# Clearing the result tiles of a block inversion on VectorE in place of GpSimd

## The chip, the cores and the metric

The kernel runs on one core of one Trainium2 chip. The metric is the device time of one execution in microseconds (us). The profile names the engines PE (TensorE), PEld (its weight loads), DVE (VectorE), ACT (ScalarE), POOL (GpSimd) and SP (SyncE, which here only issues DMAs); a q behind a name is the engine's sequencer, for example where it issues a DMA.

## What is computed

One layer of a hybrid encoder over 1024 tokens of width 1024: a windowed attention group and a bidirectional gated delta rule group read the same normalised input through one combined projection; their outputs are concatenated, projected and added; a feed-forward layer with squared ReLU follows.

```
xn   = rmsnorm(x);  proj = xn @ w_in                # q,k,v of attention; q,k,v,z,a,b of the delta rule
attn = windowed_gqa(q_a, k_a, v_a, bias, sink)      # 8 blocks of 128 queries, each sees 3 blocks of keys
gdn  = rmsnorm(rule(q,k,v,g,beta) + flip(rule(flip(...)))) * silu(z)
h    = x + concat(attn, gdn) @ w_out
out  = rmsnorm(h + relu(rmsnorm(h) @ w1)^2 @ w2)
# inside the rule, per chunk and head:
a_mat = strict_lower(beta * (k k^T) * decay)
t_mat = inverse(I + a_mat)                          # unit triangular
# t_mat multiplies the chunk's inputs; then a scan over the chunks carries a state
```

The inverses of these triangular matrices are what the changed line belongs to. There is one for every chunk, head and direction; the kernel works with 8 chunks of 128 tokens, 4 heads and 2 directions.

## The kernel before

All projections are products with the activations split in a high and a low part (`mm3`, lines L124 to L126: three matmuls for one product). The program is one list of phases. Inside a phase, `weave` interleaves two or more generators in the order in which the instructions are written down. That is not yet the order of execution: the program is built with `tile.TileContext(nc, schedule_with_timeline_sim=True)`, which lays out the queue of every engine by a simulated timeline and hands out tile buffers. On the chip each queue is then run strictly in its order, and an instruction that waits holds up all that stand behind it in its queue.

Tiles come from tagged pools with a fixed number of buffers. `pg` has 28 buffers of 128 x 1024 float32 and serves the activations, the bias tables and most of the inversion; `wh` and `wl` have three each, `pt` has 12 of half the size, and the PSUM tags `psA` and `psB` four banks each.

Two phases surround the change.

- The first weaves the rest of the input projection (`proj_conv` for v, `proj_z`, `proj_attn`) with the preparation of the delta rule: `prep` builds the matrices and stores them in DRAM (`atd`), `eliminate(0)` and `eliminate(1)` invert the 32 x 32 diagonal blocks of the forward and the backward direction on DVE (L675, L677), `diag_blocks` transposes the results (L686, L687: `ct` and `ctt`), and `invert(tt, (0, 1))` does the first two of four inversion steps.
- The second weaves `output()` (the attention, then the output projection) with `invert(tt, (2, 3))` and the two scans.

`proj_attn` begins with two casts that zero parts of the keys (L471). Each of its eight query products ends in `psA`; DVE moves it out (L494), ACT and GpSimd split it (L495, L496), and SP stores it to DRAM (`qad`, L500). `query` (L594) loads a block of queries back, by a DMA from GpSimd's queue. `bias_table` loads the attention's bias in 16 DMAs from SP's queue (L529). The scores of a block are the products of L544 and L545; DVE evicts them with the maximum (L546), ACT takes the exponentials (L558 and, for the sink, L555), and L559 is the next of DVE's small steps.

`invert` handles a pair of chunks in each step i, for both directions d (0 forward, 1 backward), in this order:

- per direction, load the matrices from `atd` (L707), take the result tile `tt[d][i]`, and clear it (L710). The result tile has the tag `pg`, except for the forward direction of i = 2 and 3, where it has `wh` and `wl`;
- ACT copies the inverted diagonal blocks into the cleared tile (L714, four copies for each direction);
- PE multiplies 32 x 32 blocks (L720), ACT moves the result (L723), PE multiplies again (L730, L734), and DVE writes the negated results into the tile (L739) and into `t64` (L746), for which ACT (L744) and GpSimd (L745) write the other parts;
- PE multiplies 64 x 64 blocks (L753), ACT moves the result (L755), PE multiplies again (L761), and DVE writes the last off-diagonal blocks (L764).

The scans read the finished tiles as the left operand of their products (L797). The clear is needed because the blocks above or below the diagonal are written by nobody else.

Of the kernel before, what the change touches and what calls it, by code (L numbers as in the profile page):

```python
# [77 lines left out]
class Block:  # L78
# [612 lines left out]
    def invert(self, tt, steps):  # L691


        nc = self.nc
        blk = lambda q: slice(32 * q, 32 * q + 32)
        ct, ctt = self.ct, self.ctt
        pairs = (((0, 1), (2, 3)), ((1, 0), (3, 2)))
        sub = ((0, 1), (3, 2))
        lo, hi = slice(0, 64), slice(64, 128)
        ends = ((lo, hi), (hi, lo))  # L700
        flat = lambda a: a.rearrange("p c h x -> p (c h) x")
        for i in steps:
            ns = slice(8 * i, 8 * i + 8)
            at = []
            for d in range(2):
                a = self.pg((P, 2, GH, P))
                nc.sync.dma_start(out=a, in_=self.atd[2 * i:2 * i + 2, :, d].rearrange("c p h x -> p c h x"))  # L707
                at.append(flat(a))
                tt[d][i] = self.pg((P, 2, GH, P)) if d or i < 2 else (self.wl if i % 2 else self.wh)((P, 2, GH, P), F32)
                nc.gpsimd.memset(tt[d][i].rearrange("p c h x -> p (c h x)"), 0.0)  # L710
            t = [flat(tt[d][i]) for d in range(2)]
            for d in range(2):
                for q in range(4):
                    nc.scalar.copy(out=t[d][blk(q), :, blk(q)], in_=ctt[d][blk(q), :, ns].rearrange("p x n -> p n x"))  # L714
            px = self.ps("psB", (P, 8, 32))
            for n in range(8):
                for j in range(2):
                    for d in range(2):
                        s, e = pairs[d][j]
                        nc.tensor.matmul(px[blk(e), n, :], at[d][blk(s), n, blk(e)], ct[d][blk(s), :, 8 * i + n],  # L720
                                         start=True, stop=True)
            x32 = self.pt((P, 8, 32))
            nc.scalar.copy(out=x32, in_=px)  # L723
            yield 1.4
            pyt, py = self.ps("psB", (P, 8, 32)), self.ps("psB", (P, 8, 32))
            for n in range(8):
                for j in range(2):
                    for d in range(2):
                        s, e = pairs[d][j]
                        nc.tensor.matmul(pyt[blk(s), n, :], x32[blk(e), n, :], ctt[d][blk(e), :, 8 * i + n],  # L730
                                         start=True, stop=True)
                for d in range(2):
                    e = sub[d][1]
                    nc.tensor.matmul(py[blk(e), n, :], ctt[d][blk(e), :, 8 * i + n], x32[blk(e), n, :],  # L734
                                     start=True, stop=True)
            t64 = self.pt((P, 8, 64))
            for d in range(2):
                for s, e in pairs[d]:
                    nc.vector.tensor_scalar(out=t[d][blk(s), :, blk(e)], in0=pyt[blk(s)], scalar1=-1.0, scalar2=None,  # L739
                                            op0=ALU.mult)  # L740
                a, b = sub[d]
                for q in (a, b):
                    c = slice(32 * (q % 2), 32 * (q % 2) + 32)
                    nc.scalar.copy(out=t64[blk(q), :, c], in_=ct[d][blk(q), :, ns].rearrange("p x n -> p n x"))  # L744
                nc.gpsimd.memset(t64[blk(a), :, 32 * (b % 2):32 * (b % 2) + 32], 0.0)  # L745
                nc.vector.tensor_scalar(out=t64[blk(b), :, 32 * (a % 2):32 * (a % 2) + 32], in0=py[blk(b)], scalar1=-1.0,  # L746
                                        scalar2=None, op0=ALU.mult)
            yield 2.4
            px = self.ps("psB", (P, 8, 64))
            for n in range(8):  # L750
                for d in range(2):
                    s, e = ends[d]
                    nc.tensor.matmul(px[e, n, :], at[d][s, n, e], t64[s, n, :], start=True, stop=True)  # L753
            xs = self.pt((P, 8, 64))
            nc.scalar.copy(out=xs, in_=px)  # L755
            yield 1.8
            py = self.ps("psB", (P, 8, 64))
            for n in range(8):
                for d in range(2):
                    s, e = ends[d]  # L760
                    nc.tensor.matmul(py[s, n, :], xs[e, n, :], t[d][e, n, e], start=True, stop=True)  # L761
            for d in range(2):
                s, e = ends[d]
                nc.vector.tensor_scalar(out=t[d][s, :, e], in0=py[s], scalar1=-1.0, scalar2=None, op0=ALU.mult)  # L764
            yield 1.8
# [612 lines left out]
```

## Time and profile before

| what | value |
|---|---|
| median of 3 runs | 1256.17 us (1255.85 to 1258.47) |
| the profiled execution | 1255.02 us |
| its span in the trace | 1253.3 us |
| mean granted TensorE clock | 0.983 |
| PE busy | 1191.6 us (95%) |
| DVE busy | 854.9 us (68%) |
| ACT busy | 621.4 us (50%) |
| POOL busy | 580.3 us (46%) |

The span runs from the first to the last instruction of the trace; the time of the execution is 1.7 us longer. Shares are averages over phases with different limits, so they do not say which engine is waited for in a given stretch. A wait in the trace is put down to the instruction that released it last. That instruction may itself have been held up by its queue, so a wait is followed back from engine to engine.

### The profile page before, as it was taken

To read this page: it belongs to the slowest core of one execution; us is meant where nothing else is said; L and a number is where in the kernel's file an instruction comes from. 1 tells how busy PE (TensorE), PEld (TensorE's weight loads), DVE (VectorE), ACT (ScalarE), POOL (GpSimd) and SP (SyncE) were. 2 spreads that over 40 slices of the span, in tenths; PEclk is the share of its full clock that TensorE was granted. 3 is DMA by queue.
4 is the path that set the end of the run, shared out by engine and by line. 5 is a ranking of instruction groups with operands and counts; after the bars stand their busy time and mean duration, and the time that the engine had idled before them with its cause. 6 is when DMAs were issued, how large, how long until landed. Compare 5 with 4: busy or idle time off the path is not lost.

```text
span 1253.3 us, 18527 instructions
## 1 busy us (share of the span) xinstructions
PE 1191.6 (95%) x6482; PEld 967.2 (77%) x6482; DVE 854.9 (68%) x1528; ACT 621.4 (50%) x1347; POOL 580.3 (46%) x488
## 2 busy tenths in 40 slices
PE   7999999899789989998999999999999999999997
PEld 5778777677568868877788888888777888888885
DVE  5667667982389986676655454544668797886976
ACT  6455688335485752125464554545545434444343
POOL 5354211362432433144573534535445665655595
PEclk9999999899889999998999999999999999999999
DMA  7134344441956678122234344443678624434323
GB/s 239 52 121 133 101 171 140 139 126 40 223 168 158 190 216 296 60 84 85 84 131 159 132 151 143 154 159 134 223 280 280 223 85 167 151 121 148 95 90 135
DMA packets 121630, 187.62 MB, mean 150 GB/s; under 512 B 11043, under 2 KB 64416, under 8 KB 121537
## 3 DMA queue, kind: packets, MB, share of 16 engines
q1 hardware_dynamic: 96708, 152.58, 37.9%
q10 hardware_dynamic: 16381, 29.67, 6.3%
q0 software_dynamic: 8448, 4.20, 1.9%
q8 instruction: 51, 0.84, 0.3%
q14 instruction: 42, 0.34, 0.1%
HBM read 122.39 MB, written 63.49 MB: 148 GB/s over the span
## 4 chain that ended last, share of the span: by engine, by line
PE 49%; DVE 6%; DMA 3%; issue 2%; POOL 1%; ACT 1%; ACTq 0%; POOLq 0%; DVEq 0%; SPq 0%
PE psA L124 8%; PE psA L125 8%; PE psA L126 8%; PE psB L126 7%; PE psB L125 7%; PE psB L124 7%; DMA pg<-sd 3%; PE psB L797 2%; DVE pg L1154 1%; DVE pt L1163 1%; DVE wr L1166 1%; PE psB L209 1%; DVE pg L1199 1%; DMA sd<-pt 0%; DVE wr L1161 0%
## 5 line engine op out<-in xcount | busy, mean ns | idle before, releaser
L124 PE MATMUL psA<-pg,wh 128*128 128x512 f32 x416 | 167.6, 404 | 2.1 <-ACT pt L458 2.1
L126 PE MATMUL psA<-pg,wl 128*128 128x512 f32 x416 | 166.9, 401 | 0.0
L125 PE MATMUL psA<-pg,wh 128*128 128x512 f32 x416 | 166.5, 400 | 0.0
L120 POOL TENSOR_TENSOR wl<-wr,wh 128x512 fp32r<-128x512 f32 x44 | 70.2, 1618 | 154.0 <-ACT wh L119 153.9
L1154 DVE TENSOR_TENSOR pg<-pg 128x512 fp32r<-128x512 f32 x112 | 122.7, 1127 | 18.8 <-ACT pg L1153 18.6
L120 POOL TENSOR_TENSOR wh<-wr,wh 128x512 fp32r<-128x512 f32 x32 | 47.9, 1518 | 131.5 <-ACT wh L119 131.5
L1071 ACT ACTIVATE pt<-pt 128x512 f32<-128x512 f32 x64 | 40.4, 632 | 122.7 <-DVE pt L1061 122.7
L125 PE MATMUL psA<-pg,pg 128*128 128x512 f32 x256 | 99.7, 391 | 0.5 <-POOL pg L120 0.5
L124 PE MATMUL psA<-pg,pg 128*128 128x512 f32 x256 | 99.0, 391 | 1.0 <-DVE pg L1199 1.0
L126 PE MATMUL psA<-pg,pg 128*128 128x512 f32 x256 | 99.7, 389 | 0.0
L120 POOL TENSOR_TENSOR pg<-wr,pg 128x512 fp32r<-128x512 f32 x48 | 73.4, 1560 | 51.0 <-ACT pg L119 51.0
L124 PEld LDWEIGHTS psA<-pg,wh 128*128 128x128 f32 x416 | 79.2, 190 | 21.3 <-ACT pt L458 2.4
L125 PEld LDWEIGHTS psA<-pg,wh 128*128 128x128 f32 x416 | 79.3, 191 | 19.7 <-issue 0.9
L126 PEld LDWEIGHTS psA<-pg,wl 128*128 128x128 f32 x416 | 79.1, 190 | 18.6
L1153 ACT CAST pg<-pg 128x512 fp32r<-128x512 f32 x112 | 67.2, 620 | 41.3 <-DMA pg<-sd 31.0
L126 PE MATMUL psB<-pg,pg 128*128 128x512 f32 x192 | 75.0, 390 | 1.3 <-DVE pg L1154 1.3
L125 PE MATMUL psB<-pg,pg 128*128 128x512 f32 x192 | 75.0, 391 | 0.8 <-POOL pg L120 0.7
L124 PE MATMUL psB<-pg,pg 128*128 128x512 f32 x192 | 74.7, 390 | 0.4 <-ACT pg L1153 0.4
L119 ACT CAST wh<-wr 128x512 fp32r<-128x512 f32 x76 | 43.6, 623 | 45.5 <-PE psA L125 24.8
L1061 DVE TENSOR_TENSOR pt<-psB,pt 128x512 f32<-128x512 f32 x39 | 26.9, 689 | 55.1 <-PE psB L126 30.1
L1061 DVE TENSOR_TENSOR pt<-psA,pt 128x512 f32<-128x512 f32 x39 | 26.8, 689 | 55.0 <-PE psA L126 39.5
L124 PEld LDWEIGHTS psA<-pg,pg 128*128 128x128 f32 x256 | 48.0, 188 | 12.6 <-DVE pg L1199 2.3
(385 smaller groups left out, 3307.7 us busy)
## 6 DMA issues: line engine op xcount, KB each, us to landing
sd<-pt ACTq DMA_DIRECT2D x112, 256.0 KB, 2.2
pg<-sd SPq DMA_DIRECT2D x112, 256.0 KB, 2.9
wr<-in_w_ffn_in SPq DMA_DIRECT2D x32, 512.0 KB, 3.8
wr<-in_w_in SPq DMA_DIRECT2D x22, 512.0 KB, 4.8
pg<-in_x SPq DMA_DIRECT2D x16, 512.0 KB, 5.4
wr<-in_w_ffn_out SPq DMA_DIRECT2D x16, 512.0 KB, 4.8
sc<-kvd SPq DMA_DIRECT2D x14, 512.0 KB, 4.1
kvd<-pt SPq DMA_DIRECT2D x16, 256.0 KB, 2.8
```

Of the source, the lines that this page charges most:

```text
L119: nc.scalar.copy(out=h, in_=raw)
L120: (eng or nc.gpsimd).tensor_tensor(out=l, in0=raw, in1=h.bitcast(F32), op=ALU.subtract)
L124: nc.tensor.matmul(ps, wh, xh, start=first, stop=False, skip_group_check=onto)
L125: nc.tensor.matmul(ps, wh, xl, start=False, stop=False, skip_group_check=onto)
L126: nc.tensor.matmul(ps, wl, xh, start=False, stop=last, skip_group_check=onto)
L209: self.nc.tensor.transpose(ps[:, i * P:(i + 1) * P], row[:, k * P:(k + 1) * P], self.ident)
L797: nc.tensor.matmul(ps[:, h - g.start, :], left(h), right[:, h, :], start=True, stop=True)
L1061: self.nc.vector.tensor_tensor(out=out, in0=in0, in1=in1, op=ALU.add)
L1071: self.nc.scalar.activation(out=c, in_=c, func=AF.Relu)
L1153: nc.scalar.copy(out=s[:, 0], in_=raw)
L1154: v.tensor_tensor(out=s[:, 1], in0=raw, in1=s[:, 0].bitcast(F32), op=ALU.subtract)
L1163: v.tensor_tensor(out=b["T2"], in0=b["B22"], in1=b["T1"], op=ALU.subtract)
```

## The change

The eight clears of L710 are issued on DVE (`nc.vector`) in place of GpSimd (`nc.gpsimd`). Tiles, sizes and everything else stay as they are.

```diff
--- before.py
+++ after.py
@@ -707,7 +707,7 @@
                 nc.sync.dma_start(out=a, in_=self.atd[2 * i:2 * i + 2, :, d].rearrange("c p h x -> p c h x"))
                 at.append(flat(a))
                 tt[d][i] = self.pg((P, 2, GH, P)) if d or i < 2 else (self.wl if i % 2 else self.wh)((P, 2, GH, P), F32)
-                nc.gpsimd.memset(tt[d][i].rearrange("p c h x -> p (c h x)"), 0.0)
+                nc.vector.memset(tt[d][i].rearrange("p c h x -> p (c h x)"), 0.0)
             t = [flat(tt[d][i]) for d in range(2)]
             for d in range(2):
                 for q in range(4):
```

## The prediction

> **What bounds the kernel now.** I read the page first, then the busy windows, then the waits of PE, and only then the line that the diff touches. From the page: the span, the engines' busy times and the chain that ended last.
>
> ```profile
> span 1253.3 us, 18527 instructions
> PE 1191.6 (95%) x6482; PEld 967.2 (77%) x6482; DVE 854.9 (68%) x1528; ACT 621.4 (50%) x1347; POOL 580.3 (46%) x488
> PE 49%; DVE 6%; DMA 3%; issue 2%; POOL 1%; ACT 1%; ACTq 0%; POOLq 0%; DVEq 0%; SPq 0%
> ```
>
> PE is busy for 1191.6 of 1253.3 us, so about 62 us of the span are PE waiting, and a change on other engines is worth what it takes from or adds to those 62 us. The next lines are the clears by their source line (buffer, count, shortest, median and longest in ns, first and last start in us, shape).
>
> ```profile
> L710 POOL MEMSET pg<- x6: 954/964/1088, 263.0 to 346.5; 128x1024 f32 x6
> L710 POOLq EVENT_SEMAPHORE  x1: 17/17/17, 295.5 to 295.5; - x1
> L710 POOL MEMSET wh<- x1: 957/957/957, 301.6 to 301.6; 128x1024 f32 x1
> L710 POOL MEMSET wl<- x1: 957/957/957, 302.5 to 302.5; 128x1024 f32 x1
> ```
>
> Eight clears of about 0.96 us, 7.7 us of GpSimd in all, and GpSimd is at 46%: its time is not what matters. What matters is who stands behind them. The waits of PE, asked for the stretch in which the inversion runs (total us, times, longest):
>
> ```profile
> PE psB L761 <- ACT pt L755: 4.9, 2, 4.4
> PE psB L753 <- DVE pt L746: 3.1, 3, 2.2
> PE psB L720 <- DMA pg<-atd: 3.1, 2, 2.1
> PE psB L720 <- DVE sc L687: 1.6, 1, 1.6
> ...
> PE psA L544 <- DMA pt<-qad: 0.8, 1, 0.8
> ```
>
> The longest, 4.4 us, names ACT, but ACT was only passing on a wait. The timelines of the four engines around it, in the order POOL, DVE, ACT, PE, SP (start, duration, engine, line, and in brackets the idle time before):
>
> ```profile
> 316.94 1.00 POOL L594 DMA_DIRECT2D pt<-qad  x1 [3.89 <-DMA pg<-biasd]
> 317.95 0.97 POOL L710 MEMSET pg<- 128x1024 f32 x1
> ```
>
> ```profile
> 312.06 0.87 DVE L746 TENSOR_SCALAR pt<-psB 32x256 f32<-32x256 f32 x2
> 318.95 0.88 DVE L739 TENSOR_SCALAR pg<-psB 32x256 f32<-32x256 f32 x2 [6.02 <-POOL pg L710]
> 319.86 2.49 DVE L494 TENSOR_SCALAR pt<-psA 128x512 f32<-128x512 f32 x4
> ```
>
> ```profile
> 318.95 2.51 ACT L714 COPY pg<-sc 32x256 f32<-32x256 f32 x4 [7.32 <-POOL pg L710]
> 321.48 0.59 ACT L755 COPY pt<-psB 128x512 f32<-128x512 f32 x1
> 322.09 2.18 ACT L495 CAST pt<-pt 128x512 fp32r<-128x512 f32 x4
> ```
>
> ```profile
> 322.12 1.68 PE L761 MATMUL psB<-pg,pt 64*64 64x64 f32 x32 [4.36 <-ACT pt L755]
> ```
>
> ```profile
> 311.65 2.73 SPq L500 DMA_DIRECT2D qad<-pt  x4
> 314.48 7.28 SPq L529 DMA_DIRECT2D pg<-biasd  x14
> 322.74 11.30 SPq L500 DMA_DIRECT2D qad<-pt  x16
> ```
>
> The reader is to see one chain. The clear of the backward tile of step i=1 stands on GpSimd behind the query load of L594, which waits 3.89 us for DMAs that have nothing to do with the inversion. Only after the clear, at 318.95, can ACT copy the diagonal blocks (L714, idle 7.32 us before) and DVE write its blocks (L739, idle 6.02 us), and behind these stand L755, for which PE waits, and four PSUM evictions (L494).
>
> **The change part by part.**
>
> *Off GpSimd.* 6 x 0.964 + 2 x 0.957 = 7.7 us. The DMA descriptors and subtractions behind them move up by at most 1 us each. Worth nothing by itself: no wait of PE in the rows above is on POOL.
>
> *On DVE.* The trace has no clear on DVE. Two rows bound it: 0.96 us, what GpSimd takes, and 1.19 us, half of the 2.38 us of two casts on DVE that write 1024 elements per partition (L471, below). I take 1.19, the nearer row because it is DVE's own; eight make 9.5 us. The Trainium skill, page "VectorE: DVE Perf Modes", section "Zero memsets can be issued as uint32 (trn2)", says that a memset takes one cycle per element whatever the type; with the 0.96 GHz of the page "Trainium Kernel Development and Optimization", section "NeuronCore Architecture", that would be an estimated 1.07 us, and 8.5 us for the eight. No run here has shown it yet.
>
> Where these 9.5 us fall is read from busy windows (PE, PEld, DVE, ACT, POOL busy, with counts, granted clock, DMA share, GB/s) and a few rows of DVE and POOL:
>
> ```profile
> 264.00:282.00 18.00, 16.52 (x74) 12.82 (x72) 17.65 (x27) 8.93 (x15) 9.18 (x9) 1.00 0.24 74
> 293.00:302.00 9.00, 9.00 (x71) 6.70 (x71) 0.36 (x1) 4.80 (x8) 5.13 (x5) 1.00 0.33 102
> 336.00:343.00 7.00, 3.00 (x74) 2.37 (x73) 4.00 (x11) 5.26 (x9) 6.41 (x9) 0.76 1.11 309
> 343.00:545.00 202.00, 187.89 (x1516) 156.55 (x1517) 165.79 (x518) 102.86 (x301) 66.73 (x58) 0.97 0.58 175
> ```
>
> ```profile
> 268.69 2.38 DVE L471 CAST pg<-zero 64x1024 fp32r<-64x1024 f32 x2
> ...
> 280.21 1.87 DVE L687 STREAM_TRANSPOSE sc<-sc 128x1024 f32<-128x1024 f32 x1
> ...
> 349.42 0.16 DVE L559 TENSOR_TENSOR nm<-nm,nm 128x4 f32<-128x4 f32 x1 [1.11 <-ACT nm L555]
> ```
>
> ```profile
> 264.95 0.96 POOL L710 MEMSET pg<- 128x1024 f32 x1 [1.00 <-DVE pt L675]
> ...
> 297.62 0.96 POOL L710 MEMSET pg<- 128x1024 f32 x1
> ```
>
> (a) *Two clears of step i=0* (the first and the second, at 263.0 and 264.95). DVE is busy for 17.65 of 18 us there with the elimination, whose last transpose (L687) ends at 280.21 + 1.87 = 282.08 and releases PE's first L720. Two clears ahead of it move it by up to 2 x 1.19 = 2.4 us; the bounds are 0 and +2.4. I take 0: PE has the projection products to run in the meantime, and the order of the queues is laid out anew with the clears in it (the trace already shows DVE running things out of the program's order, with the casts of L471 in the middle of the elimination). That cover is gone if PE's order stays as it is; then the wait of 1.6 us becomes 4.0.
>
> (b) *Three clears of i=1, 2 and 3, forward* (at 297.6, 301.6 and 302.5 on GpSimd). DVE is busy for 0.36 of 9 us at that place: 0. They can push L764 by a clear or so; its result is first read in the scan.
>
> (c) *The clear of i=1, backward.* DVE is free at 312.06 + 0.87 = 312.93. The clear also needs its buffer to be free; the trace shows no wait for that at 317.95, and the bias loads, which take buffers of the same tag and come later in the program, go out at 314.48. I take 314.5 as the latest likely time. Then the clear ends at 315.7, L714 at 315.7 + 2.51 = 318.2, L755 at 318.8, and L761 runs at about 318.85 in place of 322.12: 3.3 us. Bounds: 3.7 with the buffer at 312.9 (L755 must still wait for PE's products, which end at 322.12 - 4.36 = 317.76, and takes 0.59), 0 with the buffer at 317.9.
>
> (d) *What is late next.* After L761 come two projection products and then the score products and the L720 of step i=2, and these wait for DMAs: the `atd` loads (3.1 us of PE waiting) and the second query load (0.8). Both hang on SP's queue, and that queue is nearly full: the 14 bias loads end at 314.48 + 7.28 = 321.76, the 16 query stores start at 322.74. Earlier evictions let the stores start 0.98 us sooner, no more. At 0.68 us each (2.73 / 4, the first four) instead of 11.30 / 16 = 0.71 they save another 0.4 us; at the 0.52 of the bias loads (7.28 / 14) 3.0 more. So of 3.3 us gained at 322 between 1.0 and 3.3 are left at 342; I take 1.2, next to the stores' own rate. The rest reappears as a longer wait of L720 for `atd`: some 5 us in place of 3.1.
>
> (e) *The last two clears* (i=2 and 3, backward) (the last at 346.5) fall among the first attention blocks. One ahead of L746, which PE waits 2.2 us for, costs up to 1.2; but DVE idles 1.11 us just ahead of it, waiting for ACT's exponentials (L555). These start earlier, since the first score block comes up to 3.3 us sooner. Bounds +1.2 and -2.2; I take the hole as filled by the clear (+0.1) and half of the 2.2 us wait as gone (-1.1): -1.0.
>
> Sum: 0 + 0 - 1.2 - 1.0 = -2.2 us. The profiled execution took 1255.02 us (span 1253.3), so it would become 1252.8; the median of the runs shown, 1256.17, lies 1.15 above it, and I forecast on that: 1254.0. All of it is at the edge of what can be told from no change: 0.2% is 2.5 us.
>
> **The rivals.**
>
> *R1, the gain is kept whole.* If SP's order is laid out differently, so that stores and `atd` loads follow the earlier evictions, nothing is given back: -3.7 - 2.2 = -5.9, 1250.3. For it: the wait is real and it is a wait for a queue, not for data. Against it: SP's full queue from 314 to 334.
>
> *R2, nothing happens.* The buffer comes free only just before 317.9, or `atd` and the queries land no sooner (the DMA share is 1.11 in 336 to 343), so the whole 4.4 us turns into a DMA wait: 1256.2. Against it: the bias loads' buffers.
>
> *R3, the elimination pays.* (a) at its upper bound, DVE having no room: 1254.0 + 2.4 = 1256.4. For it: 17.65 of 18. Against it: other PE work at that place. The Trainium skill, page "Perfetto Trace Analysis", section "Optimizing Scalar/DVE Operations", says that where DVE is saturated, work may go from it to another engine, even GpSimd; by that rule this change goes the wrong way in that stretch, and the 17.65 us agree that DVE is saturated there.
>
> *R4, slower by a new order.* The program is laid out by a simulated timeline, so eight instructions that change engine can permute everything behind them. The place is the attention and scan stretch: PE idles 202.00 - 187.89 = 14.1 us there, mostly behind DVE, which is busy for 165.79. A third more idling (+4.7) outweighs -2.2 by 2.5 us and decides for slower; half more, +7.1, gives 1261.1. For it: chains of small DVE instructions with PE behind them. Against it: no row says which way a new order goes; it can also gain.
>
> **How the numbers follow.** My case 0.46 (its own range 1252.0 to 1255.5, about half of it beyond 0.2%), R1 0.16, R2 0.07, R3 0.06, R4 0.25. Faster by over 0.2%: 0.22 + 0.16 = 0.38. Within: 0.24 + 0.07 + 0.06 = 0.37. Slower: 0.25. The range runs from a little beyond R1 to R4: 1249.5 to 1261.0.
>
> **What would show it.** (c) is right if ACT's L714 of i=1 waits under 3 us for the clear and PE's wait for L755 falls from 4.4 to about 1 us. (d) is right if PE's wait for the `atd` loads grows. (a) is wrong if the wait for L687 grows from 1.6 towards 4. A clear on DVE that takes longer than 1.19 us would upset (a) and (e). The prediction fails if the order of PE's products between 260 and 545 is another one: then the rows above do not carry over.

## The result, and the profile after

| kernel | median | profiled execution | its span | mean granted clock |
|---|---|---|---|---|
| before | 1256.01 us (1254.44 to 1258.47, 4 runs) | 1255.02 us | 1253.3 us | 0.983 |
| after | 1262.96 us (1261.73 to 1264.01, 4 runs) | 1262.11 us | 1260.4 us | 0.981 |

The change makes the kernel slower: the ratio is 1.0054, with a 95% interval of 1.0037 to 1.0071, some 6.8 us. The page of after begins

```profile
span 1260.4 us, 18524 instructions
PE 1191.3 (95%) x6482; PEld 965.4 (77%) x6482; DVE 852.9 (68%) x1536; ACT 621.7 (49%) x1347; POOL 571.5 (45%) x480
```

PE is busy about as long as before (1191.3 against 1191.6 us), so in the sum the 7.1 us by which the span grew stand as PE waiting. The sum hides that some products took longer and others less; that comes below. DVE has eight instructions more, and yet its busy time did not grow. The six clears with the tag `pg`:

```profile
L710 DVE MEMSET pg<- x6: 912/912/912, 272.3 to 349.7; 128x1024 f32 x6
```

0.912 us each, shorter than on GpSimd (0.964). Now the waits of PE in the stretch where the inversion runs (260 to 420 us), which before held 4.9 us for L755 and 3.1 us for `atd`:

```profile
PE psB L720 <- DMA pg<-atd: 8.1, 2, 7.2
PE psA L585 <- ACT pt L575: 5.1, 2, 2.8
PE psA L544 <- ACT pt L575: 1.5, 1, 1.5
...
PE psB L761 <- ACT pt L755: 1.0, 2, 0.7
PE psB L753 <- DVE pt L746: 0.8, 1, 0.8
```

The wait at which the change was aimed went from 4.4 to 0.7 us, that for L746 from 2.2 to 0.8, and that for L687 is gone from the list. In their place stand a longer wait for `atd` and more waits for L575. Most of the waits for L575 hang on the last clear, that of i=3 backward. Before, GpSimd made it at 346.50; on DVE it stands among the rows of the attention and runs at 349.70. ACT's four copies into the tile (L714) wait for it, and the copies L575, for which PE waits, stand behind them in ACT's queue, which then has no gap up to the L575 of 359.86. ACT's timeline, of before and then of after:

```profile
349.30 2.54 ACT L714 COPY pg<-sc 32x256 f32<-32x256 f32 x4
```

```profile
350.65 2.61 ACT L714 COPY pg<-sc 32x256 f32<-32x256 f32 x4 [0.49 <-DVE pg L710]
353.29 0.58 ACT L575 COPY pt<-psA 128x512 f32<-128x512 f32 x1
```

From 341 to 380 PE waits 4.3 us for L575 in after, and not at all in before. (The other 2.3 us fall between 380 and 415 and are no matter of the clears: the kernel e4 below, with none moved, has 2.3 us there, too.) The timelines of DVE and PE around the clear of i=1 backward show what became of the wait that the change was aimed at:

```profile
311.88 0.91 DVE L710 MEMSET pg<- 128x1024 f32 x1 [0.28 <-issue]
```

```profile
317.50 1.15 PE L761 MATMUL psB<-pg,pt 64*64 64x64 f32 x32 [0.74 <-ACT pt L755]
...
338.56 0.28 PE L720 MATMUL psB<-pg,pg 32*32 32x32 f32 x2 [7.21 <-DMA pg<-atd]
```

The clear is done at 312.8 in place of 318.9, L761 starts 4.62 us earlier (322.12 before), and 20 us later L720 of step i=2 starts at 338.56 where it started at 339.60: only 1.04 us of it are left. The reason is SP's queue:

```profile
314.54 6.68 SPq L529 DMA_DIRECT2D pg<-biasd  x14
321.32 11.18 SPq L500 DMA_DIRECT2D qad<-pt  x16
332.54 1.06 SPq L529 DMA_DIRECT2D pg<-biasd  x2
333.70 0.89 SPq L707 DMA_DIRECT2D pg<-atd  x2
```

SP issues with hardly a pause: 14 bias loads, 16 query stores of 0.70 us each on average, two more bias loads, and only then the two loads for which L720 waits.

So much for the place of the change. The loss is 250 us further on. The waits of PE from 420 to 640 us, of before and then of after:

```profile
PE psA L910 <- DVE wr L907: 1.0, 2, 0.7
```

```profile
PE psA L910 <- DVE wr L907: 5.3, 3, 4.3
```

L910, the transposes of `out_gdn`, had not been touched. PE's timeline there, of before:

```profile
582.97 6.51 PE L209 MATMUL psB<-ident,pg 128*128 128x128 f32 x32 [3.59 <-DVE pg L205]
589.46 0.66 PE L910 MATMUL psA<-ident,wr 128*128 128x128 f32 x4
589.87 0.47 PE L124 MATMUL psA<-pg,pt 128*128 128x512 f32 x1
...
592.28 0.39 PE L125 MATMUL psA<-pg,pt 128*128 128x512 f32 x1
```

and of after:

```profile
583.59 6.25 PE L209 MATMUL psB<-ident,pg 128*128 128x128 f32 x32 [3.58 <-DVE pg L205]
594.14 1.11 PE L910 MATMUL psA<-ident,wr 128*128 128x128 f32 x4 [4.30 <-DVE wr L907]
594.91 0.78 PE L124 MATMUL psA<-pg,pt 128*128 128x512 f32 x1
...
599.21 0.39 PE L125 MATMUL psA<-pg,pt 128*128 128x512 f32 x1
```

At L209 after is 0.62 us late: over inversion, attention and scans together the change brought nothing and cost at most that in these two executions. At L910 it is 4.68 us late, and at the last row (592.28 and 599.21) 6.93. What came on top behind L910 is the clock: the ten products from that L124 to that L125 take 2.41 us before and 4.30 us after. The busy window from 592 to 596 (PE, PEld, DVE, ACT, POOL busy, granted clock, DMA share, GB/s), of before and of after, shows it:

```profile
592.00:596.00 4.00, 4.00 (x19) 3.21 (x19) 3.43 (x5) 1.24 (x2) 2.98 (x2) 1.00 0.55 152
```

```profile
592.00:596.00 4.00, 1.86 (x7) 1.67 (x8) 2.79 (x5) 0.77 (x2) 2.26 (x2) 0.53 0.01 2
```

Around and after the idle 4.30 us PE was granted 0.53 of its clock. The Trainium skill, page "TensorE: Matmul & The Clock Gate", section "Why this matters for your kernels", says that an idle gap of more than about 3 us drops PE back to half its clock; the 4.30 us and the 0.53 agree. Both kernels show the same once just ahead of this place: behind the wait of 3.59 us (3.58 in after) at L209 the granted clock was 0.50 from 583 to 587. So the loss is 4.06 us of lateness at L910 (4.68 less the 0.62 from L209), 0.36 in its own transposes (589.46 to 589.87 against 594.14 to 594.91), and 1.89 in the ten products: 6.31 us, of which the last two terms are slow clock, and nothing is made good afterwards.

Why L907 comes late is seen in the chain behind it. `out_gdn` of the last chunk takes the squares of four heads on ACT (L900), makes a factor of them in four small steps on DVE (L902 to L905), a power on GpSimd (L906), scales on DVE (L907), and PE transposes (L910). Beside it, the next phase's pass over the tokens already issues its large instructions (L966 and L214 on ACT, L215, L970 and L950 on DVE). The last square on ACT, and the first and the last small step on DVE, of before:

```profile
584.71 0.30 ACT L900 ACTIVATE scr<-pg 128x128 f32<-128x128 f32 x1
```

```profile
585.13 0.17 DVE L902 TENSOR_TENSOR sm<-sm,sq 128x4 f32<-128x4 f32 x1 [0.75 <-ACT scr L900]
...
586.38 0.15 DVE L905 TENSOR_TENSOR sm<-sm,sq 128x4 f32<-128x4 f32 x1
```

and of after:

```profile
586.45 0.69 ACT L966 ACTIVATE pg<-psB,cols 128x512 f32<-128x512 f32 x1 [0.15 <-PE psB L209]
587.03 0.30 ACT L900 ACTIVATE scr<-pg 128x128 f32<-128x128 f32 x1
```

```profile
587.65 0.15 DVE L902 TENSOR_TENSOR sm<-sm,sq 128x4 f32<-128x4 f32 x1
...
591.41 0.16 DVE L905 TENSOR_TENSOR sm<-sm,sq 128x4 f32<-128x4 f32 x1
```

The last square, which in before stands behind the first L966, stands behind the second one in after, and that waits for PE: 587.03 in place of 584.71. DVE's four small steps then stand between large ones of the token pass and take from 587.65 to 591.41, 3.76 us in place of 1.25. Nothing there is slower by itself: the queues of ACT and DVE were laid out in another order. Before had next to no room for it. Its L907,

```profile
588.73 0.68 DVE L907 TENSOR_TENSOR wr<-pg,sm 128x512 f32<-128x512 f32 x1
```

ended at 589.41, 0.05 us ahead of L910.

### The profile page after: what moved, and what is told of

Same layout as the page of the kernel before. It is cut to its first block, busy times and chain, and to the rows that moved or that the text cites. A ratio compares the mean times of both kernels' runs of the same rounds, so it can differ in the third digit from the quotient of the medians.

```text
span 1260.4 us, 18524 instructions
## 1 busy us (share of the span) xinstructions
PE 1191.3 (95%) x6482; PEld 965.4 (77%) x6482; DVE 852.9 (68%) x1536; ACT 621.7 (49%) x1347; POOL 571.5 (45%) x480
## 4 chain that ended last, share of the span: by engine, by line
PE 49%; DVE 6%; issue 3%; DMA 2%; POOL 2%; ACT 1%; POOLq 0%; ACTq 0%; DVEq 0%
PE psA L124 9%; PE psA L125 9%; PE psA L126 9%; PE psB L125 7%; PE psB L124 7%; PE psB L126 7%; PE psB L797 2%; POOL pg L120 1%; DMA pg<-sd 1%; DVE pt L1163 1%; DVE pg L1199 1%; DVE wr L1166 1%; DMA sc<-in_w_ffn_out 1%; DVE pg L215 0%; DVE pg L1154 0%
## 5 line engine op out<-in xcount | busy, mean ns | idle before, releaser
L124 PE MATMUL psA<-pg,wh 128*128 128x512 f32 x416 | 167.2, 403 | 2.2 <-ACT pt L458 2.2
L125 PE MATMUL psA<-pg,wh 128*128 128x512 f32 x416 | 166.0, 399 | 0.0
L125 PE MATMUL psA<-pg,pg 128*128 128x512 f32 x256 | 99.8, 391 | 1.7 <-POOL pg L120 1.7
L124 PE MATMUL psA<-pg,pg 128*128 128x512 f32 x256 | 99.0, 391 | 1.5 <-DVE pg L1199 0.9
L124 PEld LDWEIGHTS psA<-pg,wh 128*128 128x128 f32 x416 | 79.0, 190 | 21.2 <-ACT pt L458 2.4
L125 PEld LDWEIGHTS psA<-pg,wh 128*128 128x128 f32 x416 | 78.9, 190 | 19.5 <-issue 0.9
L125 PE MATMUL psB<-pg,pg 128*128 128x512 f32 x192 | 75.2, 391 | 0.8 <-POOL pg L120 0.7
L124 PE MATMUL psB<-pg,pg 128*128 128x512 f32 x192 | 74.7, 390 | 0.2 <-ACT pg L1153 0.2
L124 PEld LDWEIGHTS psA<-pg,pg 128*128 128x128 f32 x256 | 48.0, 188 | 13.1 <-DVE pg L1199 2.2
```

What stands on the lines that cost most here:

```text
L124: nc.tensor.matmul(ps, wh, xh, start=first, stop=False, skip_group_check=onto)
L125: nc.tensor.matmul(ps, wh, xl, start=False, stop=False, skip_group_check=onto)
```

## The experiments

The theory T1: the loss is the new order of `out_gdn`'s last chunk, which the simulated timeline lays out when times shift anywhere ahead of it; the clears on DVE cost nothing. The rival T2: the clears cost it themselves, by DVE's time. Ratios are to before as it was timed beside them, each with its 95% interval. Its median there was 1258.37 us for e1 to e4, 1258.03 for e5 to e8 and 1257.61 for e9 to e12, against 1256.01 in the table above, so it is the ratios, and not the medians, that can be compared over these groups.

**e1, one clear on DVE, that of i=1 backward.**

```diff
-                nc.gpsimd.memset(tt[d][i]...
+                (nc.vector if (i,d)==(1,1) else nc.gpsimd).memset(tt[d][i]...
```

> Kernel before, with one of the eight clears, that of i=1 backward, on DVE; PE and ACT issue in the order of before. T1 (the loss is the new order of the last chunk's out_gdn chain alone): PE's wait at L761 falls from 4.4 us to under 1, PE ends the projection some 5 us earlier, L720 then waits 5 to 7 us for atd behind SP's full queue, PE L910 has no wait at 590, and the time is that of before, 1256, at most 1 us under it. Rival, the local gain is kept: 1252. T2 (a clear on DVE costs its own 0.9 us of DVE's time): 1257.

Measured 1255.34 us, ratio 0.9984 (0.9971 to 0.9998). PE's waits from 260 to 420:

```profile
PE psB L720 <- DMA pg<-atd: 7.5, 2, 6.4
PE psB L761 <- ACT pt L755: 2.4, 3, 1.1
```

The wait at L761 is 1.1 us at most, that for `atd` grew to 6.4, and about 2 us are kept (0.16%), a little more than T1 said. This part of the change, alone, is a small gain.

**e2, one clear on DVE, that of i=3 backward** (the same edit with `(3,1)`).

> Kernel before, with the clear of i=3 backward alone on DVE. The order at the end of the inversion then comes out as after the whole change. T1: PE L910 waits about 4 us for DVE L907 near 590 us, and the time is about 6 us over before, 1262. T2 (a clear on DVE costs its own time on DVE): at most 0.9 us over before, 1257, with no wait at L910.

Measured 1267.14 us, ratio 1.0079 (1.0059 to 1.0100). PE's timeline:

```profile
587.39 2.82 PE L209 MATMUL psB<-ident,pg 128*128 128x128 f32 x12 [3.58 <-DVE pg L205]
...
597.95 1.12 PE L910 MATMUL psA<-ident,wr 128*128 128x128 f32 x4 [4.29 <-DVE wr L907]
```

The same wait of 4.3 us for L907, from a single clear that runs 240 us ahead of it. T2 would allow 0.9 us. L910 starts 10.56 us after that L209 row; in before it was 6.49, so 4.07 us are lost between the two, as in after. The whole, some 10 us, is more than the 6 that T1 gave. The traces show where the rest lies: at that L209 row e2 is already 4.42 us late (587.39 against 582.97). L720 of i=2, ahead of the moved clear, is 1.13 late (340.73 against 339.60), and the remaining 3.3 are lost behind it. A part of them is the clear's own. It runs on DVE at 354.14, and ACT's copies behind it start 5.8 us later than the 349.30 of before:

```profile
355.08 2.61 ACT L714 COPY pg<-sc 32x256 f32<-32x256 f32 x4 [0.40 <-DVE pg L710]
```

From 341 to 380 PE then waits 2.0 us for L575, in before not at all. So T1 is too strong where it says that the clears cost nothing: this one costs PE time at its own place as well, through what waits for it and not through DVE's 0.9 us.

**e3, after with one more ordering.** The first L966 of the token pass is put behind the last square of `out_gdn` on ACT; the clears stay on DVE.

```diff
-            nc.scalar.activation(out=scr, in_=o[:, h, :], func=AF.Square, accum_out=so[:, h:h + 1])
+            self.square = nc.scalar.activation(out=scr, in_=o[:, h, :], func=AF.Square, accum_out=so[:, h:h + 1]).ins
...
-            nc.scalar.activation(out=b12, in_=ps, func=AF.Copy, scale=self.w_ffn[:, k:k + 1])
+            first = nc.scalar.activation(out=b12, in_=ps, func=AF.Copy, scale=self.w_ffn[:, k:k + 1]).ins
+            k or self.tc.add_manual_dep(first, self.square.name, ...)
```

> Kernel after, all eight clears on DVE, with one more ordering: the first L966 of the token pass is put behind the last square (L900) of out_gdn on ACT. T1: the 4.3 us wait of PE L910 is gone or under 1 us, and the time is within 1 us of before, 1255 to 1257. T2 (the clears on DVE cost the loss themselves): stays at 1262 to 1263.

Measured 1257.87 us, ratio 0.9998 (0.9985 to 1.0011): the loss is gone. PE's timeline:

```profile
589.48 0.60 PE L910 MATMUL psA<-ident,wr 128*128 128x128 f32 x4
```

L910 starts with no wait, though all eight clears are on DVE. T2 falls as the cause of the loss. The order is not that of before, where the first L966 stands ahead of the last square; it is another good one.

**e4, before with the same ordering**, the control.

> Kernel before with the same ordering of L966 behind L900, the clears on GpSimd: the control of the run above. T1: its order there is as good as before, so 1255 to 1257. If the ordering by itself gained some 6 us (1250), the run of after with it would say nothing on T1.

Measured 1258.18 us, ratio 0.9998 (0.9984 to 1.0012). The ordering by itself is worth nothing where the order was good already; in e3 it was worth the 0.54%.

**e9, the order without any moved clear.** The clears are on GpSimd as before, and every second query store is issued by ACT's queue (`(nc.sync, nc.scalar)[g].dma_start` in L500), which shifts the simulated times too. Its partner e8 has the same stores and the ordering of e4.

> Kernel of e4 (clears on GpSimd) with every second query store on ACT's queue: control of e7. T1: PE's wait at L761 for the clear on GpSimd stays at 4 us or becomes shorter only if the query loads ahead of the clear on GpSimd's queue, which wait for these stores, come earlier; the time is 0 to 2 us under e4's 1258.2.

> Kernel of e8 without the ordering of L966 behind L900: every clear on GpSimd as before, every second query store on ACT's queue. The planner then puts the last two squares of out_gdn's last chunk behind ACT's L966, as in after, though no clear is moved. T1 (the order alone costs): PE L910 waits about 4 us near 590, and the time is 5 to 7 us over e8's 1258.5, about 1264. T2 (the clears on DVE are needed for the loss): as e8, 1258 to 1259.

Measured e8 1258.53 us, 1.0008 (0.9995 to 1.0020), and e9 1262.61 us, 1.0037 (1.0023 to 1.0052). PE's timeline of e9:

```profile
595.09 0.98 PE L910 MATMUL psA<-ident,wr 128*128 128x128 f32 x4 [4.27 <-DVE wr L907]
```

The wait for L907 is there again, with GpSimd clearing all eight tiles. It costs 0.29% against e8 by the ratios, 3.7 us (the two were timed in different groups), less than the 5 to 7 us expected. So the clears on DVE are neither needed for the loss (e9) nor enough for it (e1, e3).

**e10, four clears on DVE**, those of i=0 and 1 in both directions (the condition `i<2`; the word "forward" in its name is wrong), with no ordering by hand.

> Kernel before with four of the eight clears on DVE, those of i=0 and 1, and nothing ordered by hand; the end of the inversion keeps the order of before. T1: no wait of PE L910, and the time is that of before or 1 to 2 us under it, as in e1: 1255 to 1257. T2 (each clear on DVE costs 0.9 us): 3 to 4 us over before, about 1261.

Measured 1255.49 us, ratio 0.9978 (0.9966 to 0.9989). PE's timeline:

```profile
589.90 0.66 PE L910 MATMUL psA<-ident,wr 128*128 128x128 f32 x4
```

No wait at L910, and a gain of 0.22%, 2.8 us, a little more than T1 gave, where T2 gave a loss of 3 to 4. All eight with a good order (e3, 0.9998) do not keep this gain. The clears of i=2 and 3 and the ordering are the difference; in the trace of e3 PE waits 2.8 us for L575 from 341 to 380, in that of e10 not at all. Whether that is the whole of it isn't shown.

**e5 to e8, e11 and e12: is it SP's queue that takes the local gain back?** e5 is e3 with the `atd` loads of i=2 and 3 on ACT's queue (`(nc.scalar if i > 1 else nc.sync).dma_start` in L707); e6 is e4 with the same.

> Kernel of e3 (all clears on DVE, L966 ordered behind L900), with the four loads of atd for i=2 and 3 issued by ACT's queue in place of SP's. T1 (what PE gained by the earlier clear is given back because SP's queue is full with 14 bias loads and 16 query stores): the two loads of i=2 issue some 8 to 10 us earlier than SP's 332.9, the 6.4 us wait of L720 for atd falls under 1.5 us, and the time falls 3 to 5 us under e3's 1257.9, to about 1253 to 1255. Rival (the transfer itself, or the buffer that it fills, is late, not the queue): the wait stays 5 us or more and the time is e3's. Second rival: the wait goes, and what comes next (ACT's copies, the query loads) takes its place: time within 1 us of e3's.

> Kernel of e4 (clears on GpSimd, L966 ordered behind L900) with the same four loads on ACT's queue: the control. T1: PE still waits 4.4 us at L761 for the clear on GpSimd, and the wait of L720 (1.4 and 1.4 us in e4) goes: at most 2 us under e4's 1258.2, so about 1256 to 1258. If it falls as far as e5, the queue alone was worth the gain and the clears nothing.

Measured e5 1257.10 us, 0.9998 (0.9985 to 1.0012), e6 1255.32 us, 0.9986 (0.9974 to 0.9998). ACT and PE of e5 (timeline of ACT, then PE's waits from 260 to 420):

```profile
318.95 0.46 ACTq L707 DMA_DIRECT2D pg<-atd  x1
```

```profile
PE psA L544 <- DMA pt<-qad: 9.0, 1, 9.0
```

The first load went out at 318.95 (332.9 expected of SP), and the wait of L720 is gone, but the second rival holds: the score products L544 now wait 9.0 us for queries, whose 16 stores stand in the same queue of SP. Taking the loads out of the queue is not enough; the stores are what fills it. The control e6, with GpSimd clearing, came out at the lower end of what was expected and no slower than e5: with the loads moved, the clears on DVE bring nothing.

e7 is e3 with every second query store on ACT's queue (the edit of e9).

> Kernel of e3 with every second query store (L500) issued by ACT's queue in place of SP's, the loads left on SP's. T1: SP reaches the loads of i=2 about 5 us earlier (half of its 16 stores of 0.69 us before them go), L720's wait of 6.4 us falls to 1 to 2 us, and the time falls 2 to 4 us under e3's 1257.9. Rival: ACT pays for its 14 issues before 340 and its copies come late: the time is e3's or over it.

Measured 1254.78 us, ratio 0.9973 (0.9958 to 0.9989): faster than before by 0.27% (3.4 us). Against e3, which stood at 0.9998 in other rounds, that would be 0.25%, but the two intervals just overlap. SP's timeline and PE's waits of e7:

```profile
329.66 1.10 SPq L707 DMA_DIRECT2D pg<-atd  x2
```

```profile
PE psB L720 <- DMA pg<-atd: 5.1, 2, 4.5
```

The loads issue at 329.66, 3.2 us earlier than in e3 (332.86), and L720 starts 1.7 us earlier (335.39 against 337.08): half of what the queue gave reaches PE. The wait at L720 is 4.5 us in place of 6.4 in e3, not the 1 to 2 expected. Its control e8, with the same stores and the clears on GpSimd, gains nothing. Its waits from 260 to 420 still begin with

```profile
PE psB L761 <- ACT pt L755: 4.4, 2, 4.2
```

So with the stores split the clears on DVE are worth 0.35% (e7 against e8, timed together), and with all stores on SP's queue nothing (e3 against e4). That both must give way before PE gains does not follow: e1, e6 and e10 show gains of 0.14 to 0.22% with one of the two alone, though the intervals of e1 and e6 reach to 0.9998. The Trainium skill, page "DMA: Bandwidth & Descriptors", section "Issuing engines are not separate DMA queues", says that issuing from several engines saves only the issuing time, usually small beside the transfer. Here that time, 11.18 us for 16 stores, held the loads back for which PE waited.

e11 is e3 with the 16 bias loads on ACT's queue (`self.nc.scalar.dma_start` in L529), e12 is e7 with the same.

> Kernel of e3 with the 16 bias loads (L529) issued by ACT's queue in place of SP's, the query stores left on SP's. If SP's queue holds back both the loads of atd and the queries: SP's 16 stores start at once, some 6 us earlier, L720's wait for atd and the wait for the queries fall to 1 to 2 us, and the time is 3 to 5 us under e3's 1257.9. Rival: ACT pays 16 issues of 0.5 us (8 us) in this stretch and its copies come late: e3's time or over it.

> Kernel of e7 (all clears on DVE, ordered, every second query store on ACT's queue) with the 16 bias loads on ACT's queue as well. If SP's queue is still the last wait in e7 (4.5 us at L720): 1 to 3 us under e7's 1254.8. Rival: 28 stores and 16 loads issued by ACT take some 20 us of it, and its copies for the inversion come late: over e7's time.

Measured e11 1257.76 us, 1.0001 (0.9986 to 1.0016), e12 1261.73 us, 1.0033 (1.0020 to 1.0046). The rivals hold: from 310 to 345 PE of e12 waits

```profile
PE psA L544 <- DMA pt<-qad: 5.2, 2, 4.3
PE psB L761 <- ACT pt L755: 3.6, 1, 3.6
```

ACT has to issue the DMAs itself, and its copy L755 comes late again, by nearly as much as the clear on GpSimd had made it. The best versions run are e7 and e10.

## Why the prediction was wrong

The forecast was 1254.0 us, and the time came out above the range. Its steps:

- *Price of the clear*: taken as 1.19 us, bounded below by 0.96. It is 0.912, outside the bounds: the casts of L471 were the wrong neighbour, and GpSimd's own row was not a floor. By the rule that the prediction took from the Trainium skill (page "VectorE: DVE Perf Modes", section "Zero memsets can be issued as uint32 (trn2)"), one cycle per element, it would have been the estimated 1.07; the row is shorter, and the measurement decides.
- *(a)* right. The wait of 1.6 us for L687 did not grow; it is gone, since PE's order changed there. *(b)* no loss of PE's was found at those three clears.
- *(c)* right in its chain, too small in its size: the buffer was free at once, so the clear ran at 311.88 and not at 314.5, and L761 came 4.62 us earlier in place of 3.3. The bound of 3.7 was passed because PE's products ahead of it ended a microsecond earlier too, at 316.76 in place of 317.76.
- *(d)* right in kind: SP's queue takes the gain back. The sum kept 1.2 us; at L720 1.04 were left. The wait for `atd` grew to 8.1 us in place of the 5 forecast.
- *(e)* half right: the wait of 2.2 us for L746 fell to 0.8, but L585 and L544 wait 6.6 us for L575 in after. The sum took the clear as filling a hole of DVE and did not follow it to ACT's L714 and to L575 behind it. Of the gain of 1.0 nothing is left at 583 us.
- *R4* is the step that failed, in its chance and in its place. The mechanism named there, a new order laid out by the simulated timeline, decided the result. But it had 0.25, and it was put into the attention and scan stretch, 343 to 545 us, where the two traces come out alike on the whole. It struck at 590, in a chain of small steps just ahead of PE's transposes. Its price, 7.1 us on top of -2.2, came out as 6.3, near it by luck, since it was sized from another stretch; 2.3 us of the 6.3 are slow clock, which no step had in it. The range ended at 1261.0, just under what R4 itself gave.

What the sum assumed without saying so was that behind the inversion everything keeps its order. The prediction's own condition for failing, "the order of PE's products between 260 and 545", looked at the wrong stretch. The order did change in it, too (the L720 of i=1 start in two groups, at 301.36 and 305.26, in place of one at 302.81), and on the whole that neither gained nor cost much. The row that could have warned is the L907 of before, which ended 0.05 us ahead of L910: a chain of ten instructions over four engines with hardly any slack, at a seam between two phases. The waits of PE could not show it: the 1.0 us for L907 are two waits at earlier chunks, and at the last one there was none.

## What to carry to other kernels

Where a scheduler lays out the queues, a change of one instruction's engine is a change of the whole order behind it: compare the queues instruction by instruction to the end of the program, and look first at chains of small instructions that end with little slack at a seam between phases. A loss found far from the edit is tested by forcing a good order there, with the same forcing on the old kernel as control; here that separated a loss of 0.5% from an edit whose gain and cost at its own place cancel (0.9998). When a wait is taken away and PE soon waits for a DMA, look at how full the issuing queue is: a second queue helps only if its engine has the time (e7 against e11 and e12). And an instruction moved to an engine with room must be followed to what waits for it there, as L714 and L575 did for the last clear.

## What the hardware showed that was not expected

- A clear of 128 x 1024 float32 took 0.912 us on DVE, 5% less than on GpSimd.
- A wait of 4.30 us, where before had none, cost PE 6.3: the granted clock was 0.53 around it, and the ten products behind it took 4.30 us in place of 2.41.
- SP took 0.70 us on average for each 64 x 512 store that it issued and 0.48 us for each 32 x 2 x 384 load (11.18 / 16, 6.68 / 14). Thirty in a row are 18 us of a queue, with PE behind it.
